# Four edits at the MLP openings of a two-layer trunk: where operand T4 is summed, from which pair the modulation steps run, which engine adds some squares, and where one statistic stands

## The chip, the cores and the metric

One core of a Trainium2 chip runs the program. The metric is the device time of one execution in microseconds (us), as a median over runs. TensorE (PE) multiplies matrices, VectorE (DVE), ScalarE (ACT) and GpSimd (POOL) work on tiles, and SyncE (SP) issues most of the DMAs. Each engine runs its own instructions in a fixed order and waits on semaphores for the others.

## The reference

A trunk of two layers over 1024 latent tokens and 256 context tokens, width 1024. Every sub-layer is preceded by an RMSNorm with a scale and a shift that depend on a conditioning vector (the modulation), and is added with a gate that depends on it too.

```python
def rms_norm(x, g):
    y = xf * lax.rsqrt(jnp.mean(xf * xf, axis=-1, keepdims=True) + EPS)
    return y * g
def sqrelu_mlp(h, w1, w2):
    return jnp.square(jax.nn.relu(h @ w1)) @ w2
```

Layer 0 mixes with an mLSTM head group beside a gated convolution, layer 1 with attention; the MLP has 4096 hidden columns. The change lies in the two MLPs and just ahead of that of layer 0.

## The kernel before, in words

**Arithmetic.** A number is split into a high and a low part of the type fp32r (`split`: the high part by a copy, L101; the low part by a subtraction, L102), and a product takes three matmuls (`mm3`, L337 to L339). The tokens lie in three blocks: 0 and 1 hold 512 latent tokens each, 2 the 256 of the context; a tile xT holds a block with the features on the partitions, 8 chunks (kt or m) of 128.

**The first MLP matrix (fc1).** `fast_fc1` multiplies 2x2 blocks by the method of Strassen and Winograd: 7 products instead of 8. A pair p is two blocks of 128 hidden columns; there are 16. For each pair the products come in the order 1, 2, 6, 5, 7, 3, 4 (layer 0 puts 8, the context's, ahead of 4), each of 4 x 3 matmuls of 128x512. For product i the token side is an operand tb[i], a sum or a difference of quarters of the normalised tokens, made once; the weight side is a sum of raw weight blocks (`ssum` or `s`, by `comb`, L853, on DVE), split into `w` by ACT (L101) and DVE (L102). Products 1 and 2 (and 8 and 9 of the context) of the first three pairs run early, while the other operands are still being made; products 6, 5, 7, 3, 4 of pair 0 follow. `after` copies or squares the results (L950, L957, L958), combines them (`c<-c` and `c<-ps,u`, L853), and spills them to DRAM (L962, L946, on SP).

**Operand T4.** `Blocks.t4` makes tb[4] = tb[2] - tb[6] just behind product 5 of pair 0: for each of 4 chunks two subtractions and an addition on DVE (12 of L853, `c<-tb` and `c<-c`), and a split. Product 4 of pair 0 is its first user.

**Modulation of layer 1.** While fc1 of layer 0 runs, `ada_steps` (L196 on) computes the modulation of layer 1 in 12 chunks of 5 steps, 60 in all: four steps each load a quarter of 0.5 MB into the tile `araw` (L203, on SP) and add it up on DVE (two or four of L211 and L213), the fifth transposes the sums on TensorE (L218) and reduces them (L220, L221, DVE). Here `araw` has a single buffer, so each load waits until DVE is done with the quarter before. `extra` takes a step behind products 2, 5, 3 and 4 of each pair that is not early, 61 chances in all; what is left is done by `step(ada1[0], 1000)` behind fc1.

**Squares and statistics.** `Norm.square` has ACT square a chunk (L281, L284) and DVE add it up (L285); behind the eighth it splits the sum into ahi and alo (L101, L102). `Norm.stat` sums these over the partitions on TensorE with a matrix of ones (L294, L295), and ACT makes rstd of it (L297, L298). Ahead of fc1 of layer 0, a loop over the blocks 2, 0, 1 and the chunks m adds the mixer's output to the stream (`add_gated`, L348) and takes squares; the statistic of block 2 is asked for behind chunk (0, 1).

**fc2.** `fast_fc2` begins with four matmuls with a tile of zeros (L1106) that open its accumulators. Its tokens come back from DRAM, 2 MB for each of the blocks 0 and 1 (`unpark`, 4 DMAs on SP each, `xT<-park`).

**Order.** The program is written as straight code; a list scheduler in the framework then fixes each engine's order from its own model of times and the dependences. A few instructions are kept in program order (`pe_`, `dve_`, ...). So an edit at one place moves instructions at others.

Of the kernel before, what the change touches and what calls it, by code (L numbers as in the profile page):

```python
# [11 lines left out]
F32 = mybir.dt.float32  # L12
F32R = mybir.dt.float32r
AF = mybir.ActivationFunctionType
ALU = mybir.AluOpType
# [4 lines left out]
P = 128  # L20
# [26 lines left out]
def trunk(ctx, tc, a, out):  # L47
    nc = tc.nc
    sp, act, dve, pool, pe = nc.sync, nc.scalar, nc.vector, nc.gpsimd, nc.tensor

    def opened(name, bufs=1, space=None, side=None):
        kw = {"space": space} if space is not None else {}
        if side is not None:
            kw["side"] = side
        return tc.tile_pool(name=name, bufs=bufs, reuse_waits="tile", **kw)
# [13 lines left out]
    def psum():  # L69
        return ps_pool.tile([P, 512], F32, name="ps", tag="ps")  # L70


    ident = const.tile([P, P], F32, name="ident")
    make_identity(nc, ident)
    ones_f = const.tile([P, P], F32, name="ones_f")
# [148 lines left out]
    def step(it, n=1):  # L224
        for _ in range(n):
            if next(it, "end") == "end":
                return
# [290 lines left out]
    for half in (1, 0):  # L518
        n = 264
        wc = load_cols(w_in, 1024 + 264 * half, n)  # L520
        for tt in range(NTT):
# [10 lines left out]
            if half:  # L532
                gv = po[:, 248:264].rearrange("p (d f h) -> p d f h", d=2, f=2)
                bv = gbias.rearrange("p (d f h) -> p d f h", d=2, f=2)
                for f, dst in ((0, ig_all), (1, fg_all)):
                    o = dst[:, tt, :]
# [119 lines left out]
    for which, dst in ((0, qT), (1, kT)):  # L656
        for i in range(2):
            w = load_split(kt_view(w_in, which * 256 + i * P, P), [KT, P])
            for b in range(3):
                t0, n = TBS[b]  # L660
# [191 lines left out]
    def comb(out, a_, b_, op, eng=None):  # L852
        (eng or dve).tensor_tensor(out=out, in0=a_, in1=b_, op=op)  # L853
# [266 lines left out]
    class Blocks:  # L1120
# [9 lines left out]
        def temp(self):  # L1130
            return self.p.tile([P, 512], F32, name="t", tag="t", bufs=4)
# [75 lines left out]
            for k in range(4):  # L1207
                self.put(3, k, self.b22[k])

        def t4(self, hi4, lo4, temp):  # L1210

            self.tb[4] = hi4, lo4
            f = lambda ap: ap.bitcast(F32)
            for k in range(4):
                t, u = temp(), temp()
                for o, x in ((t, 0), (u, 1)):
                    comb(o, f(self.tb[2][x][:, k]), f(self.tb[6][x][:, k]), ALU.subtract)
                comb(t, t, u, ALU.add)
                self.put(4, k, t)

    act_big = lambda shape: act_pool.tile(shape, F32R, name="tb", tag="act")

# [20 lines left out]
    x2ctx, x1ctx, nctx, x0ctx, lctx, actx = (ExitStack() for _ in range(6))  # L1243
# [1 line left out]
    shift = mod[0][:, 24:32, :]  # L1245
    zctx = ExitStack()
    zero = zctx.enter_context(opened("zero", 1, side="right")).tile([P, P], F32R, name="zero")
    act.activation(out=zero, in_=ones_f, func=AF.Copy, scale=0.0)
    x1 = x_of(x1ctx, 1)
    np_ = nctx.enter_context(opened("nrm", 1, side="right"))  # L1250
    xT = [x_of(x0ctx, 0), x1, x_of(x2ctx, 2)]
# [2 lines left out]
    nbs = [Norm(np_, xT[b], b, g2, shift, tbufs=4) for b in range(3)]  # L1254
# [12 lines left out]
    blocks = Blocks(np_, g2, shift, [np_.tile([P, 512], F32, name="b11", tag="b11", bufs=4) for _ in range(4)], act_big, lambda shape: big(tbp)(shape))  # L1267
    parked2 = {}
    parked2[1], part1 = park_in_parts(1, 2)
    for b in (2, 0, 1):  # L1270
        for m in range(KT):
            py = held.pop(0) if b == 2 else psum()
            if b < 2:
                mlstm_out(b, m, py)
            add_gated(xT, b, m, py, 0, 2)
            nbs[b].square(m)
            if (b, m) == (0, 1):
                parked2[2] = park(2, 2)
                nbs[2].stat()
                h2 = nbs[2].apply()  # L1280
                x2ctx.close()
            if (b, m) == (1, 0):
                nbs[0].stat()
                blocks.first(nbs[0])
                parked2[0] = park(0, 2)
            if b == 1:
                part1(m)
                if m >= 4:
                    blocks.ahead(nbs[1], m - 4)
# [6 lines left out]
    wp, raw_tile = Later(), lambda shape, e=0: raw_pool.tile(shape, F32, name="raw", tag="raw")  # L1296
# [5 lines left out]

    def begin(p, i, room):
        if i == 5 and fourth and p == room[1] // 3:
            t4 = fourth.pop()
            blocks.t4(t4[:, 0], t4[:, 1], lambda: wp.tile([P, 512], F32, name="c", tag="c", bufs=room[2]))

    fourth = []

    def extra(p, i, room):  # L1310
        begin(p, i, room)
        if i in (2, 5, 3, 4):
            step(ada1[0])

    def end():
        blocks.put22()
        nctx.close()
        x1ctx.close()
        t4 = lctx.enter_context(opened("tb4", 1)).tile([P, 2, 4, 512], F32R, name="tb4")
        ap = actx.enter_context(opened("adp", 1, side="right"))  # L1320
        ada1.append(ada_steps(ap, 1, (4, 0, 5, 6, 1, 7, 8, 2, 9, 10, 3, 11), lambda ch: ch < 4, lambda: ap.tile([P, 2, 512], F32, name="araw", tag="araw")))
        wp.p = actx.enter_context(opened("fc1w", 1, side="right"))
        return t4
# [3 lines left out]
    fast_fc1(0, blocks, wp, hid_d, 3, raw_tile, 3, {1: stats, 3: lambda: blocks.t1(nbs[1]), 6: lambda: blocks.t3(nbs[1]), 11: lambda: fourth.append(end())},  # L1327
             (3, 2, 6, None), extra, ctx=h2, hid_c=hid_c, slots=slots)
    step(ada1[0], 1000)
    actx.close()  # L1330
    lctx.close()

# [67 lines left out]
    with opened("rope", 1, side="right") as rp:  # L1400
# [127 lines left out]
        k = 12 - TAIL  # L1528
# [16 lines left out]
    with opened("s", 2, PSUM) as scp, opened("st", 2, PSUM) as stp, opened("av", 2, PSUM) as avp, \  # L1545
# [94 lines left out]
        k = 12  # L1640
# [79 lines left out]
    def end():  # L1720
        blocks.put22()
        rctx.close()
        x1ctx.close()
        t4 = actx.enter_context(opened("tb4", 1, side="right")).tile([P, 2, 4, 512], F32R, name="tb4")
        wp.p = actx.enter_context(opened("fc1w", 1, side="right"))
        return t4

# [67 lines left out]
```

## Time and profile before

| what | value |
|---|---|
| median of 3 runs | 2891.22 us (2886.96 to 2892.35) |
| the profiled execution | 2892.08 us |
| its span | 2890.3 us |
| mean granted TensorE clock | 0.984 |
| PE busy | 2787.5 us, 96% |
| DVE, ACT, POOL busy | 70%, 52%, 24% |

A clock of 1.00 in a row is 2.4 GHz, 0.50 is 1.2 GHz. A line of a timeline has the start, the duration (of xN instructions together), the engine, the line of the code, the operation, its tiles and shapes, and in brackets the idle time of the engine before it and what ended it. Matmuls overlap, so their pitch is the distance of their starts, not their duration.

### The profile page before, as it was taken

How to read it: one execution, taken by the hardware profiler on the slowest of the kernel's cores; microseconds unless marked ns; L12 is line 12 of the kernel's file. 1: busy time of each engine (PE TensorE's matmuls, PEld its weight loads, DVE VectorE, ACT ScalarE, POOL GpSimd, SP SyncE). 2: the span in 40 equal slices, each digit the busy share in tenths (PEclk: the TensorE clock that was granted, in tenths of full speed). 3: DMA queues.
4: the chain of work that ended last, by engine and by line, in shares of the span. 5: the costliest groups of instructions: out<-in, count | busy, mean ns of one | idle time of the engine just before them, and what ended most of it. 6: DMA issues, size and time to landing. Idle time of an engine off the chain costs nothing.

```text
span 2890.3 us, 39559 instructions
## 1 busy us (share of the span) xinstructions
PE 2787.5 (96%) x14603; PEld 2307.4 (80%) x14603; DVE 2009.4 (70%) x3376; ACT 1496.9 (52%) x2576; POOL 686.8 (24%) x566
## 2 busy tenths in 40 slices
PE   7999999988999999999999989999999999999999
PEld 4788998876888888888888967777777788878887
DVE  6445581778767679778877767777755966578876
ACT  5311122765444454444556578888875655544443
POOL 2222313620000000000135545555554000000000
PEclk9999999999999999999999989999999999999999
DMA  7121652535665684324232310000025254484432
GB/s 241 51 70 42 202 157 59 177 115 151 210 182 176 190 300 159 131 81 146 100 121 77 92 41 19 15 19 19 19 74 178 84 186 155 139 295 160 146 98 106
DMA packets 194835, 360.21 MB, mean 125 GB/s; under 512 B 15206, under 2 KB 83666, under 8 KB 194642
## 3 DMA queue, kind: packets, MB, share of 16 engines
q1 hardware_dynamic: 179970, 312.59, 32.2%
q0 software_dynamic: 14672, 45.10, 6.0%
q8 instruction: 115, 1.88, 0.3%
q14 instruction: 78, 0.64, 0.1%
HBM read 260.53 MB, written 97.10 MB: 124 GB/s over the span
## 4 chain that ended last, share of the span: by engine, by line
PE 56%; DVE 7%; ACT 6%; DMA 4%; issue 2%; POOL 1%; SPq 0%; DVEq 0%; ACTq 0%; POOLq 0%
PE ps L339 14%; PE ps L338 14%; PE ps L337 14%; PE av L92 4%; PE st L92 3%; DMA araw<-in_ada_w_dram 2%; PE s L92 2%; ACT pt L92 2%; ACT pf L92 2%; ACT of L92 1%; PE ps L508 1%; PE ps L509 1%; PE ps L510 1%; DMA hid<-c 1%; DVE aacc L213 1%
## 5 line engine op out<-in xcount | busy, mean ns | idle before, releaser
L338 PE MATMUL ps<-w 128*128 128x512 f32 (+1 forms) x1152 | 424.6, 369 | 0.9 <-DVE w L102 0.9
L339 PE MATMUL ps<-w 128*128 128x512 f32 (+1 forms) x1152 | 423.7, 369 | 0.0
L337 PE MATMUL ps<-w 128*128 128x512 f32 (+1 forms) x1152 | 406.1, 369 | 1.5 <-ACT w L101 1.5
L337 PE MATMUL ps<-tb,w 128*128 128x512 f32 x883 | 349.5, 397 | 9.7 <-ACT w L101 7.8
L338 PE MATMUL ps<-tb,w 128*128 128x512 f32 x888 | 350.7, 395 | 1.9 <-DVE tb L92 1.9
L339 PE MATMUL ps<-tb,w 128*128 128x512 f32 x888 | 347.8, 395 | 0.8 <-DVE w L102 0.8
L348 DVE SCALAR_TENSOR_TENSOR xT<-ps,mod,xT 128x512 f32<-128x512 f32 (+1 forms) x392 | 256.4, 695 | 97.8 <-PE ps L339 86.0
L92 DVE TENSOR_REDUCE nm<-s 128x1 f32<-128x512 f32 x372 | 217.7, 600 | 107.1 <-PE s L92 102.1
L101 ACT CAST w<-ssum 128x512 fp32r<-128x512 f32 x253 | 153.9, 619 | 250.6 <-PE ps L339 232.2
L92 POOL TENSOR_TENSOR pt<-pf,pt 128x1024 fp32r<-128x1024 f32 x96 | 230.6, 2402 | 170.4 <-ACT pt L92 170.2
L92 PE MATMUL av<-pt,vst 128*128 128x512 f32 (+1 forms) x960 | 257.5, 394 | 0.8 <-POOL pt L92 0.8
L338 PEld LDWEIGHTS ps<-w 128*128 128x128 f32 x1152 | 216.8, 188 | 41.0 <-DVE w L102 1.3
L337 PEld LDWEIGHTS ps<-w 128*128 128x128 f32 x1152 | 216.2, 188 | 41.2 <-ACT w L101 1.8
L339 PEld LDWEIGHTS ps<-w 128*128 128x128 f32 x1152 | 216.3, 188 | 38.8
L92 PEld LDWEIGHTS av<-pt,vst 128*128 128x128 f32 (+1 forms) x960 | 159.7, 171 | 55.9 <-POOL pt L92 1.3
L337 PEld LDWEIGHTS ps<-tb,w 128*128 128x128 f32 x883 | 167.4, 190 | 46.1 <-ACT w L101 8.9
L895 POOL DMA_DIRECT2D raw<-in_mlp_w_dram x70 | 62.3, 890 | 594.9 <-DVE w L102 278.5
L92 ACT ACTIVATE pf<-st 128x1024 f32<-128x1024 f32 x160 | 164.3, 1027 | 75.4 <-PE st L92 74.2
L339 PEld LDWEIGHTS ps<-tb,w 128*128 128x128 f32 x888 | 167.9, 189 | 40.2 <-DVE w L102 2.3
L338 PEld LDWEIGHTS ps<-tb,w 128*128 128x128 f32 x888 | 168.7, 190 | 37.4 <-DVE tb L92 2.8
L213 DVE SCALAR_TENSOR_TENSOR aacc<-araw,cw,aacc 128x512 f32<-128x512 f32 x196 | 145.7, 775 | 71.5 <-DMA araw<-in_ada_w_dram 70.6
L102 DVE TENSOR_TENSOR w<-ssum,w 128x512 fp32r<-128x512 f32 x253 | 171.5, 686 | 23.9 <-ACT w L101 23.3
(387 smaller groups left out, 6581.5 us busy)
## 6 DMA issues: line engine op xcount, KB each, us to landing
hid<-c SPq DMA_DIRECT2D x224, 256.0 KB
tf<-hid SPq DMA_DIRECT2D x112, 512.0 KB
araw<-in_ada_w_dram SPq DMA_DIRECT2D x72, 512.0 KB
raw<-in_mlp_w_dram POOLq DMA_DIRECT2D x70, 512.0 KB, 4.9
park<-xT SPq DMA_DIRECT2D x32, 512.0 KB
xT<-park SPq DMA_DIRECT2D x32, 512.0 KB
w2e<-in_mlp_w_dram SPq DMA_DIRECT2D x32, 512.0 KB
w2o<-in_mlp_w_dram SPq DMA_DIRECT2D x32, 512.0 KB
```

The source lines that it names most:

```text
L92: return lambda *args, **kw: tc.keep_in_program_order(op(*args, **kw))
L101: (hi_eng or act.copy)(out=hi, in_=src)
L102: (lo_eng or pool).tensor_tensor(out=lo, in0=src, in1=hi.bitcast(F32), op=ALU.subtract)
L213: dve.scalar_tensor_tensor(out=accs[w], in0=r[:, k, :], scalar=c, in1=accs[w], op0=ALU.mult, op1=ALU.add)
L337: pe1.matmul(ps, whi, hhi, start=start, stop=False, skip_group_check=goes_on)
L338: pe.matmul(ps, whi, hlo, start=False, stop=False, skip_group_check=goes_on)
L339: pe.matmul(ps, wlo, hhi, start=False, stop=stop, skip_group_check=goes_on)
L348: dve.scalar_tensor_tensor(out=xT[b][:, m, :], in0=ps[:, 0:n], scalar=mod[layer][:, gate * 8 + m, w:w + 1], in1=xT[b][:, m, :], op0=ALU.mu ...
L508: pe.matmul(ps[:, 0:n], hhi, whi, start=kt == 0, stop=False)
L509: pe.matmul(ps[:, 0:n], hhi, wlo, start=False, stop=False)
L510: pe.matmul(ps[:, 0:n], hlo, whi, start=False, stop=kt == KT - 1)
L895: pool.dma_start(out=r, in_=kt_view(w1, (2 * p + e) * P, P))
```

## The change

1. T4 is summed on TensorE, in both layers. For each of the 4 chunks four matmuls of 128x512 add plus and minus identities times the high and low parts of tb[2] and tb[6] in a PSUM bank, and the split reads that bank. The identities are scaled by ACT (L1222). Layer 0 uses the tile `zero` as minus and fills it with zeros behind fc1 (L1333).
2. `extra` takes a modulation step only from pair 1 on. That leaves 58 chances for 60 steps: the last quarter of chunk 11 and its transposes are now taken by `step(ada1[0], 1000)`.
3. The squares of block 1 with odd m are added on POOL (four of L285).
4. The statistic of block 2, its norm and its parking are asked for behind chunk (0, 3).

```diff
-        def t4(self, hi4, lo4, temp):
+        def t4(self, hi4, lo4, signs):
             self.tb[4] = hi4, lo4
-            f = lambda ap: ap.bitcast(F32)
             for k in range(4):
-                t, u = temp(), temp()
-                for o, x in ((t, 0), (u, 1)):
-                    comb(o, f(self.tb[2][x][:, k]), f(self.tb[6][x][:, k]), ALU.subtract)
-                comb(t, t, u, ALU.add)
+                t = psum()
+                for n, (i, x) in enumerate(((2, 0), (2, 1), (6, 0), (6, 1))):
+                    pe.matmul(t, signs[i // 6], self.tb[i][x][:, k], start=n == 0, stop=n == 3)
                 self.put(4, k, t)
+    def with_signs(p, minus=None):
+        signs = [p.tile([P, P], F32R, name="plus"), minus or p.tile([P, P], F32R, name="minus")]
+        for t, v in zip(signs, (1.0, -1.0)):
+            act.mul(out=t, in_=ident, mul=v)
+        return p.tile([P, 2, 4, 512], F32R, name="tb4"), signs
...
-            nbs[b].square(m)
-            if (b, m) == (0, 1):
+            nbs[b].square(m, pool if b == 1 and m % 2 else dve)
+            if (b, m) == (0, 3):
                 parked2[2] = park(2, 2)
                 nbs[2].stat()
...
     def extra(p, i, room):
         begin(p, i, room)
-        if i in (2, 5, 3, 4):
+        if p >= 1 and i in (2, 5, 3, 4):
             step(ada1[0])
...
     step(ada1[0], 1000)
+    act.activation(out=zero, in_=ones_f, func=AF.Copy, scale=0.0)
```

**How it moves instructions, first place: ahead of block 2's statistic.** DVE before, around the split of the sum of squares of block 2 (128x256); xT_5555 is block 0.

```order
L348 SCALAR_TENSOR_TENSOR xT_5555<-ps,mod_118,xT_5555 128x512
L285 TENSOR_TENSOR acc<-acc,sq 128x256
L348 SCALAR_TENSOR_TENSOR xT_5555<-ps,mod_118,xT_5555 128x512
L285 TENSOR_TENSOR acc<-acc,sq 128x256 x3
L101 CAST ahi<-acc 128x256
L102 TENSOR_TENSOR alo<-acc,ahi 128x256
L285 TENSOR_TENSOR acc<-acc,sq 128x512
L348 SCALAR_TENSOR_TENSOR xT_5555<-ps,mod_118,xT_5555 128x512
```

DVE now (block 0 is xT_5554):

```order
L348 SCALAR_TENSOR_TENSOR xT_5554<-ps,mod_118,xT_5554 128x512
L285 TENSOR_TENSOR acc<-acc,sq 128x256
L348 SCALAR_TENSOR_TENSOR xT_5554<-ps,mod_118,xT_5554 128x512
L285 TENSOR_TENSOR acc<-acc,sq 128x256 x3
L348 SCALAR_TENSOR_TENSOR xT_5554<-ps,mod_118,xT_5554 128x512
L101 CAST ahi<-acc 128x256
L102 TENSOR_TENSOR alo<-acc,ahi 128x256
L285 TENSOR_TENSOR acc<-acc,sq 128x512
```

One more gated addition of block 0 stands ahead of the split; on TensorE, 23 more matmuls of the mixer's output stand ahead of L294, which uses it (row 2638 before, 2661 now).

**Second place: the opening of fc1.** DVE before, in products 6, 5 and 7 of pair 0:

```order
L102 TENSOR_TENSOR w<-s_6331,w 128x512
L853 TENSOR_TENSOR ssum<-raw 128x512
L853 TENSOR_TENSOR c<-tb 128x512 x6
L853 TENSOR_TENSOR s_6331<-raw,s_6331 128x512
L213 SCALAR_TENSOR_TENSOR aacc_6495<-araw,cw,aacc_6495 128x512
L102 TENSOR_TENSOR w<-ssum,w 128x512
L853 TENSOR_TENSOR c<-c 128x512 x3
L102 TENSOR_TENSOR w<-s_6331,w 128x512
L102 TENSOR_TENSOR w<-raw,w 128x512
L853 TENSOR_TENSOR c<-tb 128x512 x2
L102 TENSOR_TENSOR tb_6406<-c,tb_6406 128x512 x2
L213 SCALAR_TENSOR_TENSOR aacc_6495<-araw,cw,aacc_6495 128x512
```

DVE now, at the split of T4 (tb_6408 is tb[4], `ps` a PSUM bank):

```order
L853 TENSOR_TENSOR ssum<-raw 128x512
L102 TENSOR_TENSOR tb_6408<-ps,tb_6408 128x512
L853 TENSOR_TENSOR ssum<-ssum,raw 128x512
L853 TENSOR_TENSOR ssum<-raw 128x512
L102 TENSOR_TENSOR tb_6408<-ps,tb_6408 128x512 x2
L102 TENSOR_TENSOR w<-ssum,w 128x512
L102 TENSOR_TENSOR tb_6408<-ps,tb_6408 128x512
L213 SCALAR_TENSOR_TENSOR aacc_6613<-araw,cw,aacc_6613 128x512
```

TensorE now, behind product 5 of pair 0:

```order
L339 MATMUL ps<-tb,w 128x512
L1216 MATMUL ps<-tb,plus 128x512 x2
L1216 MATMUL ps<-tb,zero 128x512 x2
L1216 MATMUL ps<-tb,plus 128x512 x2
L1216 MATMUL ps<-tb,zero 128x512 x2
L1216 MATMUL ps<-tb,plus 128x512 x2
L1216 MATMUL ps<-tb,zero 128x512 x2
L1216 MATMUL ps<-tb,plus 128x512 x2
L1216 MATMUL ps<-tb,zero 128x512 x2
L337 MATMUL ps<-tb,w 128x512
```

The 12 combs are gone from DVE, and 16 matmuls stand in TensorE's order.

**Third place: the end of fc1 of layer 0.** TensorE before, at its last modulation transposes, some 60 rows ahead of fc2's first matmul (L1106 is row 4937):

```order
L337 MATMUL ps<-tb,w 128x512
L338 MATMUL ps<-tb,w 128x512
L339 MATMUL ps<-tb,w 128x512
L218 MATMUL ps<-ident,aacc_9599 128x128 x4
L337 MATMUL ps<-h2h,w 128x256
L338 MATMUL ps<-h2l,w 128x256
L339 MATMUL ps<-h2h,w 128x256
```

TensorE now; h2h is the context's operand, and L1106 opens fc2:

```order
L337 MATMUL ps<-tb_6408,w 128x512
L338 MATMUL ps<-tb_6408,w 128x512
L339 MATMUL ps<-tb_6408,w 128x512
L339 MATMUL ps<-h2h,w 128x256
L218 MATMUL ps<-ident,aacc_9767 128x128 x4
L1106 MATMUL ps<-w,zero 128x512 x4
L337 MATMUL ps<-w 128x256
```

DVE now, in the same stretch (`c<-c` are the combinations of pair 15's results, `w` weights of fc2):

```order
L213 SCALAR_TENSOR_TENSOR aacc_9767<-araw,cw,aacc_9767 128x512 x2
L853 TENSOR_TENSOR c<-c 128x512
L102 TENSOR_TENSOR w<-w2e,w 128x512
L853 TENSOR_TENSOR c<-c 128x512 x3
L102 TENSOR_TENSOR w<-tf,w 128x512
L213 SCALAR_TENSOR_TENSOR aacc_9767<-araw,cw,aacc_9767 128x512 x2
L102 TENSOR_TENSOR w<-w2o,w 128x512
L213 SCALAR_TENSOR_TENSOR aacc_9767<-araw,cw,aacc_9767 128x512 x2
L220 TENSOR_REDUCE asum<-ps 128x4
```

SP now, in the same stretch (xT_9895 and xT_9894 are the blocks 1 and 0 for fc2, `hid` and `hidc` spills of pair 15):

```order
L92 DMA xT_9895<-park_5577 128x1024 x3
L962 DMA hid_6024<-c 128x512
L203 DMA araw<-in_ada_w_dram 128x2x512
L962 DMA hid_6024<-c 128x512
L946 DMA hidc_6028<-c 128x512
L962 DMA hid_6024<-c 128x512 x4
L1043 DMA tf<-hid_6021 128x1024
L92 DMA xT_9894<-park_5872 128x1024 x4
L203 DMA araw<-in_ada_w_dram 128x2x512
L92 DMA xT_9899<-park_5680 128x512 x4
```

The last transposes now stand between fc1 and fc2, behind two pairs of L213 at the end of DVE's pair 15, and the last `araw` stands on SP behind the spills and four transfers of xT.

## Rows read from the trace of the kernel before

**Rows 1.** The page: busy time and share of the span of each engine.

```profile
PE 2787.5 (96%) x14603; PEld 2307.4 (80%) x14603; DVE 2009.4 (70%) x3376; ACT 1496.9 (52%) x2576; POOL 686.8 (24%) x566
```

**Rows 2.** Busy time by stretch, from the end of the mixer's output (620) to the opening of fc1 of layer 0: columns PE, PEld, DVE, ACT, POOL busy (and instructions), clock, DMA share, GB/s.

```profile
620.00:640.00 20.00, 16.90 (x70) 13.16 (x70) 19.26 (x27) 14.42 (x26) 8.96 (x6) 0.83 0.21 72
...
660.00:680.00 20.00, 17.30 (x84) 13.74 (x83) 19.99 (x35) 13.11 (x24) 1.77 (x2) 0.91 0.40 126
```

**Rows 3.** Timeline of PE at the statistic of block 2.

```profile
582.56 0.55 PE L294 MATMUL ps<-ahi,ones_r 128*128 128x256 f32 x1 [5.61 <-DVE ahi L101]
...
586.75 0.63 PE L337 MATMUL ps<-mT,whi 128*128 128x512 f32 x1
587.18 0.44 PE L338 MATMUL ps<-mT,whi 128*128 128x512 f32 x1
```

**Rows 4.** Timeline of PE in the opening of fc1 of layer 0: the matmuls that it waited for, and two at the end of a stretch at the lower clock.

```profile
629.36 0.79 PE L337 MATMUL ps<-tb 128*128 128x512 f32 x1 [3.07 <-ACT tb L101]
...
668.66 0.50 PE L92 MATMUL ps<-tb,w 128*128 128x512 f32 x1 [1.92 <-ACT w L101]
...
677.54 0.50 PE L339 MATMUL ps<-tb,w 128*128 128x512 f32 x1 [0.78 <-DVE w L102]
...
687.94 0.79 PE L337 MATMUL ps<-tb,w 128*128 128x512 f32 x1 [5.05 <-ACT w L101]
...
692.38 0.63 PE L337 MATMUL ps<-tb,w 128*128 128x512 f32 x1
...
700.14 0.63 PE L218 MATMUL ps<-ident,aacc 128*128 128x128 f32 x4 [1.29 <-DVE aacc L213]
...
709.48 0.50 PE L337 MATMUL ps<-tb,w 128*128 128x512 f32 x1 [2.76 <-ACT w L101]
```

**Rows 5.** Timeline of DVE in the same stretch: the combs of T4, the weight sum and the low part that follow them, and two waits for modulation loads.

```profile
671.92 3.69 DVE L853 TENSOR_TENSOR c<-tb 128x512 f32<-128x512 f32 x6
...
677.40 1.89 DVE L853 TENSOR_TENSOR c<-c 128x512 f32<-128x512 f32 x3
...
680.41 1.29 DVE L853 TENSOR_TENSOR c<-tb 128x512 f32<-128x512 f32 x2
...
684.69 0.69 DVE L853 TENSOR_TENSOR c<-c 128x512 f32<-128x512 f32 x1
...
686.55 0.69 DVE L853 TENSOR_TENSOR ssum<-ssum,raw 128x512 f32<-128x512 f32 x1
...
697.97 0.75 DVE L213 SCALAR_TENSOR_TENSOR aacc<-araw,cw,aacc 128x512 f32<-128x512 f32 x1 [4.54 <-DMA araw<-in_ada_w_dram]
...
716.54 1.41 DVE L213 SCALAR_TENSOR_TENSOR aacc<-araw,cw,aacc 128x512 f32<-128x512 f32 x2 [3.09 <-DMA araw<-in_ada_w_dram]
```

**Rows 6.** Timeline of SP's queue: the issues of the two loads that the last two rows of group 5 waited for.

```profile
692.86 0.38 SPq L203 DMA_DIRECT2D araw<-in_ada_w_dram  x1
...
711.58 0.39 SPq L203 DMA_DIRECT2D araw<-in_ada_w_dram  x1
```

**Rows 7.** POOL: the group of its 128x512 multiplications in fp32 (L789), by form (busy us, mean ns); and the timelines of DVE and POOL at one place before fc1 of layer 1, where both work on SBUF.

```profile
L789 POOL TENSOR_TENSOR gso<-gso,hs 128x512 f32<-128x512 f32 x10 | 12.7, 1276 | 6.3 <-ACT rs L791 4.9 <-DVE hs L777 1.0 <-ACT mT L101 0.4
...
2197.70 2.40 POOL L102 TENSOR_TENSOR wlo<-raw,whi 128x1024 fp32r<-128x1024 f32 x1 [2.60 <-ACT whi L101]
...
2198.26 2.38 DVE L285 TENSOR_TENSOR acc<-acc,sq 128x512 f32<-128x512 f32 x1 [0.75 <-ACT sq L284]
```

**Rows 8.** Layer 1: timeline of PE at its last wait in the opening of fc1, and of DVE at its first T4 combs.

```profile
2284.88 0.50 PE L337 MATMUL ps<-tb,w 128*128 128x512 f32 x1 [0.76 <-ACT u L950]
2285.22 0.40 PE L338 MATMUL ps<-tb,w 128*128 128x512 f32 x1
2285.45 0.40 PE L339 MATMUL ps<-tb,w 128*128 128x512 f32 x1
...
2284.79 3.09 DVE L853 TENSOR_TENSOR c<-tb 128x512 f32<-128x512 f32 x5
```

**Rows 9.** The end of fc1 of layer 0, timeline of PE: the last modulation transposes, fc1's last matmul, fc2's first.

```profile
1054.52 0.60 PE L218 MATMUL ps<-ident,aacc 128*128 128x128 f32 x4
...
1065.95 0.28 PE L339 MATMUL ps<-h2h,w 128*128 128x256 f32 x1
1066.07 1.09 PE L1106 MATMUL ps<-w,zero 128*128 128x512 f32 x4
```

**Rows 10.** The same place, timeline of DVE: the wait for the last quarter, and the last combination of pair 15.

```profile
1049.52 0.75 DVE L213 SCALAR_TENSOR_TENSOR aacc<-araw,cw,aacc 128x512 f32<-128x512 f32 x1 [2.35 <-DMA araw<-in_ada_w_dram]
...
1070.76 0.68 DVE L853 TENSOR_TENSOR c<-c 128x512 f32<-128x512 f32 x1
```

**Rows 11.** The same place, timeline of SP's queue: the last modulation load, four transfers of xT, and the spills of pair 15 and the load behind them.

```profile
1045.39 0.38 SPq L203 DMA_DIRECT2D araw<-in_ada_w_dram  x1
...
1062.10 3.50 SPq L92 DMA_DIRECT2D xT<-park  x4
1065.99 0.96 SPq L962 DMA_DIRECT2D hid<-c  x2
...
1071.75 0.39 SPq L1043 DMA_DIRECT2D tf<-hid  x1
```

**Rows 12.** Busy time by stretch from the end of fc1 on, columns as in group 2.

```profile
1060.00:1080.00 20.00, 20.00 (x147) 18.98 (x146) 13.57 (x22) 13.30 (x24) 0.00 (x0) 1.00 1.03 377
1080.00:1420.00 340.00, 340.00 (x1794) 291.25 (x1793) 275.45 (x451) 151.55 (x266) 0.00 (x0) 1.00 0.36 127
```

More of the change, by code (lines that the diff above doesn't have):

```diff
@@ L1247, in trunk @@
     zero = zctx.enter_context(opened("zero", 1, side="right")).tile([P, P], F32R, name="zero")
-    act.activation(out=zero, in_=ones_f, func=AF.Copy, scale=0.0)
     x1 = x_of(x1ctx, 1)
@@ L1304, in begin @@
         if i == 5 and fourth and p == room[1] // 3:
-            t4 = fourth.pop()
-            blocks.t4(t4[:, 0], t4[:, 1], lambda: wp.tile([P, 512], F32, name="c", tag="c", bufs=room[2]))
+            t4, signs = fourth.pop()
+            blocks.t4(t4[:, 0], t4[:, 1], signs)
     fourth = []
@@ L1318, in end @@
         x1ctx.close()
-        t4 = lctx.enter_context(opened("tb4", 1)).tile([P, 2, 4, 512], F32R, name="tb4")
+        t4 = with_signs(lctx.enter_context(opened("tb4", 1)), zero)
         ap = actx.enter_context(opened("adp", 1, side="right"))
@@ L1723, in end @@
         x1ctx.close()
-        t4 = actx.enter_context(opened("tb4", 1, side="right")).tile([P, 2, 4, 512], F32R, name="tb4")
+        t4 = with_signs(actx.enter_context(opened("tb4", 1, side="right")))
         wp.p = actx.enter_context(opened("fc1w", 1, side="right"))
```

## The prediction

> **What bounds the kernel now.** The page first: TensorE is busy for 2787.5 us of the 2890.3 us span, DVE for 70% [rows 1]. So TensorE sets the end, and an edit is worth what it takes from TensorE's idle time or its time at the lower clock, or adds to its work. DVE counts only where TensorE waits for it. I therefore looked for TensorE's waits, and at DVE and SP only there.
>
> At the statistic of block 2 TensorE stands for 5.61 us until DVE has split the sum of squares, and then runs at the lower clock: the matmul at 586.75 comes 0.43 us before the next [rows 3]. In the opening of fc1 of layer 0 DVE is busy for 19.99 of 20 us [rows 2], and TensorE waits 1.92, 0.78, 5.05, 1.29 and 2.76 us for weights, or modulation sums, that DVE makes or makes possible [rows 4], 11.80 us together. The longest lies behind the T4 combs [rows 5]. In the same stretch 3.07 us go at the first product of block 1 [rows 4]. From the opening of fc1 of layer 1 on hardly anything is left to win: the last wait there is 0.76 us [rows 8]. And the end of fc1 of layer 0 is seamless: last modulation transposes at 1054.52, last fc1 matmul at 1065.95, first fc2 matmul at 1066.07 [rows 9], then 340.00 busy of 340 us [rows 12]. That last place is the one to watch.
>
> **The change part by part.**
>
> *A, the statistic of block 2.* TensorE now has 24 matmuls of the mixer's output (m = 2 and 3) ahead of the one that waits, 24 x 0.23 (the pitch of [rows 8]) = 5.5 us of work that is there anyway and fills the 5.61 us. Without the gap the clock has no reason seen here to fall: of the ten matmuls from 582.9 to 587.18, at a pitch of 0.43 instead of 0.23, 2 us come back [rows 3]. The split itself waits for one more gated addition, whose matmuls are ahead of it on TensorE, so a part of a microsecond may remain. Value -7.5, bounds -8 and -4. Parking and the context's norm start some 6 us later; block 2's operand is first used by products 8 and 9 in fc1, some 50 us on, which covers that.
>
> *B, squares on POOL.* Four additions leave DVE (0.6 us each) for POOL, where the nearest form takes 1.28 us [rows 7]. The last of them, which completes the sum, stands on POOL behind four splits (7.2 us) and a weight issue; DVE's split of the sum follows it, and on TensorE the block's statistic stands behind more of the context's short matmuls than before, about 2 us later by their number. So T2, T3 and T6 begin later by that, at a time when TensorE has products of the early pairs to do. The gap of 3.07 us waits for ACT, and stays. Against it speaks how the two engines meet: while POOL split 128x1024 for 2.40 us, an addition of DVE that took 0.69 elsewhere took 2.38 [rows 7]. If each POOL square holds DVE so for 1.28 us, four cost DVE 5.1 us and spare it 2.4, net 2.7, in a stretch where DVE is full (19.26 of 20 [rows 2]). Value +0.5, bounds -1 and +3. The Trainium skill, "GPSIMD Engine Reference", section Specifications, says the same of its cause: the two engines share their SBUF interfaces, and contend when DVE's instruction has two SBUF inputs; by it the upper bound, +3, would stand in place of +0.5 and the sum would be 2.5 us higher.
>
> *C, the opening of layer 0.* T4 took DVE 3.69 + 1.89 + 1.29 + 0.69 = 7.6 us [rows 5], less 0.3 for overlaps. The modulation steps of pair 0 took some 5 of L211 and L213, 0.75 us each [rows 5], 3.5 us more. All that stood ahead of the sum that the wait of 5.05 us ended on. With about 10 us off DVE there, that wait goes, with 2.2 us at the lower clock behind it (11 matmuls up to 692.38 [rows 4], 0.2 us each). Most of 0.78 goes too. The wait of 1.92 lies ahead of T4 and stays in part. Those of 1.29 and 2.76 do not go: DVE stands for `araw` for 4.54 and 3.09 us, each 5 us behind the issue (692.86 to 697.97, 711.58 to 716.54 [rows 5, 6]); with one buffer that wait moves with the steps to pair 1. Of 11.8 idle and about 5.3 at the lower clock, I leave 4.5 and 3.2, so 9.4 come back. TensorE pays 16 matmuls of 128x512 at 0.23, the pitch of [rows 8]: 3.7. Value -5.7, bounds -10 (everything but the 1.92 gone) and 0 (the waits on `araw` take the place of those on DVE).
>
> *D, the opening of layer 1.* The same 16 matmuls, 3.7 us. The combs stand on DVE from 2284.79 on, when TensorE's last wait, 0.76 us for ACT, is just over [rows 8], so nothing waits for them. Half of the matmuls can lie in that 0.76. Value +2.9, bounds +2 and +4.
>
> *E, the last two steps.* The last transposes now stand on TensorE between fc1's last matmul and fc2's first; everything of fc2 is queued behind them, and needs nothing of them. In the time of before, TensorE arrives at 1066.2. The third quarter's additions stand on DVE behind the combinations of pair 15, the last of which began at 1070.76 [rows 10], and a split: they run at about 1071.9 to 1073.3. Only then is the single buffer free. On SP the last load also stands behind pair 15's spills, a load of `tf` at 1071.75, and four transfers of xT that take 3.50 us to issue [rows 11], so it goes out at about 1075.8. From issue to use a load took 4.1 [rows 10, 11] to 5.1 us [rows 5, 6]: landing at 1080 to 1081, two additions of 0.7, and TensorE goes on at about 1082. With a delay of one microsecond for the 2 MB of xT just ahead of it (377 GB/s move there at a DMA share of 1.03 [rows 12]), the stall is 17 us. Behind waits of 5 us TensorE lost 1.9 to 2.2 us at the lower clock; I add 2. Nothing gives this back: TensorE is busy for all of the next 340 us [rows 12]. Value +19. Lower bound: xT does not stand in the way, load at 1073.3, 4.1 us, 1.4 us: a stall of 12.6, with clock +14. Upper bound: xT's 2 MB, 5.6 us at 377 GB/s, are drained first, and the third load is late by 2: 24 us, with clock +26.
>
> The Trainium skill, "DMA: Bandwidth & Descriptors", section Anatomy of one DMA, gives an estimate for a transfer: 2.0 us and the bytes at 436 GB/s, 3.2 us for 0.5 MB. The rows show 4.1 to 5.1, so the trace does not agree; by the page E would be 2 us less.
>
> **Sum.** -7.5 + 0.5 - 5.7 + 2.9 + 19 = +9.2 on the profiled execution of 2892.1 us: 2901.3. That execution lies 0.9 us over the median, so 2900.4.
>
> **The rivals.**
>
> *R1, no stall at the end.* The order on TensorE is fixed, but the last load could land before TensorE arrives, if quarter three is done inside pair 15 and SP is early. For it: before, the last transposes came 11.5 us ahead of fc1's end. Against it: two more steps, and the additions stand behind combinations that need the last product. A to D alone: -9.8, 2881.4, faster.
>
> *R2, short stall, full relief.* E at its lower bound, +14, and C at -9, A -7.5, B +0.5, D +2.5: +0.5, 2891.7. For it: DVE and SP reach the end of pair 15 earlier if TensorE does. It decides when the last load goes out before 1074.
>
> *R3, long stall.* E at +26 with C at -5: +17, 2908, slower. For it: the DMA share at 1060 to 1080; against it: TensorE, which needs weights and hidden columns from the same DMA engines there, is busy for 20.00 of 20 us.
>
> *R4, T4 gives nothing back.* The waits in the opening were for `araw` and weights, not for T4: C 0 and B +3 with E +19: +17, 2908, slower. It decides if DVE still has no free time behind product 5.
>
> **How the numbers follow.** The forecast has 0.48, R1 0.15, R2 0.22, R3 0.09, R4 0.06. A measurement of this kernel tells about 0.2%, 5.8 us, from no change: faster is under 2885.4, slower over 2897.0. Of the forecast, with its spread of some 6 us, three quarters are slower and the rest the same; R1 is faster; of R2 three quarters are the same and the rest faster; R3 and R4 are slower. Faster 0.20, same 0.29, slower 0.51. The range: to R1's 2881 at the low end would take in all; I leave half of R1 out, 2883, and above R3 and R4, 2912.
>
> **What would show it.** A: no wait of over 1 us ahead of the 128x256 statistic. C: no wait of 5 us behind product 5 of pair 0, and DVE with free time there. D: no more waits in layer 1's opening, 16 more matmuls. E: one wait of 13 to 24 us for `aacc` at the last transposes, a lower clock behind it, and DVE waiting for `araw` just before. I am wrong if that wait is under 10 us, or if the opening keeps its 12 us of waits.

## The result, and the profile after

The changed kernel takes 2916.66 us (2911.75 to 2922.1, 4 runs) against 2890.56 us on the same chip: ratio 1.0089 (95% interval 1.0077 to 1.010), 26 us slower. The forecast was 2900.4 us, slower; the time lies above its range. The execution profiled after is the slowest of the four, 2922.1 us with a span of 2920.3, so the ledger below sums to 30 us, 4 more than the medians differ.

TensorE's waits of the kernel after, from its timeline, and fc2's first matmuls:

```profile
583.86 0.38 PE L294 MATMUL ps<-ahi,ones_r 128*128 128x256 f32 x1 [1.15 <-DVE ahi L101]
600.54 0.79 PE L294 MATMUL ps<-ahi,ones_r 128*128 128x512 f32 x1 [2.20 <-DVE ahi L101]
625.80 0.79 PE L337 MATMUL ps<-tb 128*128 128x512 f32 x1 [3.42 <-ACT tb L101]
...
667.64 0.50 PE L339 MATMUL ps<-tb,w 128*128 128x512 f32 x1 [1.86 <-DVE w L102]
698.64 0.50 PE L339 MATMUL ps<-tb,w 128*128 128x512 f32 x1 [1.08 <-DVE w L102]
732.83 0.39 PE L339 MATMUL ps<-h2h,w 128*128 128x256 f32 x1 [2.19 <-DVE w L102]
...
928.93 0.50 PE L337 MATMUL ps<-tb,w 128*128 128x512 f32 x1 [1.58 <-DVE c L853]
973.96 0.39 PE L339 MATMUL ps<-h2h,w 128*128 128x256 f32 x1 [1.88 <-DVE w L102]
...
1029.74 0.39 PE L339 MATMUL ps<-h2h,w 128*128 128x256 f32 x1 [2.55 <-DVE w L102]
...
1068.17 0.28 PE L339 MATMUL ps<-h2h,w 128*128 128x256 f32 x1
1092.14 1.09 PE L218 MATMUL ps<-ident,aacc 128*128 128x128 f32 x4 [23.69 <-DVE aacc L213]
1092.88 2.06 PE L1106 MATMUL ps<-w,zero 128*128 128x512 f32 x4
```

Read beside [rows 3] and [rows 4], the wait of 5.61 us has shrunk to 1.15, that of 5.05 us is gone, and 3.42 stands for 3.07. New are the waits of 1.6 to 2.6 us from 928 on, where the kernel before had hardly any, and the one of 23.69 us at the last transposes; [rows 9] have none there. The four L1106 take 2.06 us instead of 1.09, at a granted clock of 0.50 from 1092 to 1095; with the transposes and what follows that is some 1.5 us.

DVE of the kernel after, from its timeline, just ahead of three of the waits from 928 on, and at the wait of 23.69 us:

```profile
925.53 2.74 DVE L213 SCALAR_TENSOR_TENSOR aacc<-araw,cw,aacc 128x512 f32<-128x512 f32 x4 [5.31 <-DMA araw<-in_ada_w_dram]
...
972.55 0.75 DVE L213 SCALAR_TENSOR_TENSOR aacc<-araw,cw,aacc 128x512 f32<-128x512 f32 x1 [3.05 <-DMA araw<-in_ada_w_dram]
...
1025.14 2.08 DVE L213 SCALAR_TENSOR_TENSOR aacc<-araw,cw,aacc 128x512 f32<-128x512 f32 x3 [3.17 <-DMA araw<-in_ada_w_dram]
...
1068.70 1.54 DVE L213 SCALAR_TENSOR_TENSOR aacc<-araw,cw,aacc 128x512 f32<-128x512 f32 x2 [2.87 <-DMA araw<-in_ada_w_dram]
...
1071.36 1.89 DVE L853 TENSOR_TENSOR c<-c 128x512 f32<-128x512 f32 x3
...
1076.81 1.54 DVE L213 SCALAR_TENSOR_TENSOR aacc<-araw,cw,aacc 128x512 f32<-128x512 f32 x2 [2.19 <-DMA araw<-in_ada_w_dram]
...
1090.45 1.54 DVE L213 SCALAR_TENSOR_TENSOR aacc<-araw,cw,aacc 128x512 f32<-128x512 f32 x2 [7.42 <-DMA araw<-in_ada_w_dram]
```

SP of the same run, from its timeline (w2e and w2o are fc2's weights):

```profile
1050.96 0.57 SPq L1034 DMA_DIRECT2D w2e<-in_mlp_w_dram  x1
...
1052.60 0.94 SPq L1034 DMA_DIRECT2D w2e<-in_mlp_w_dram  x2
1053.65 1.97 SPq L1034 DMA_DIRECT2D w2o<-in_mlp_w_dram  x3
1055.66 0.52 SPq L1034 DMA_DIRECT2D w2e<-in_mlp_w_dram  x1
1056.23 0.43 SPq L1034 DMA_DIRECT2D w2o<-in_mlp_w_dram  x1
...
1058.19 0.38 SPq L203 DMA_DIRECT2D araw<-in_ada_w_dram  x1
...
1070.27 0.38 SPq L203 DMA_DIRECT2D araw<-in_ada_w_dram  x1
...
1076.89 2.65 SPq L92 DMA_DIRECT2D xT<-park  x4
1080.48 0.38 SPq L203 DMA_DIRECT2D araw<-in_ada_w_dram  x1
```

So DVE stands for a modulation load for 3 to 5 us shortly before it makes what TensorE waits for at 928.93, 973.96 and 1029.74. The last three loads take 10.5, 6.5 and 10.0 us from issue to use, where those of [rows 5, 6, 10, 11] took 4.1 to 5.1. They are serial: each goes out only after the additions that free the buffer. The first of the three goes out behind eight loads of fc2's weights, 4 MB, the last behind four transfers of xT, 2 MB.

Where TensorE gains and loses, stretch by stretch. The stretches before and after run between the same matmuls or the same copies of products (L950), so a column is a difference of two starts:

| stretch | forecast | measured |
|---|---|---|
| start of the execution to 546 | | +1.1 |
| A, to block 0's statistic (605.96, now 600.54) | -7.5 | -6.5 |
| B, to product 1's copy of the first opening pair (674.00, now 671.47) | +0.5 | +2.9 |
| C, to the copy at 698.88 (now 691.61) | -5.7 for all of fc1 | -4.7 |
| C, to fc1's last matmul (1065.95, now 1068.17) | | +9.5 |
| E, to L1106 (1066.07, now 1092.88) | +19 | +24.6 |
| from there to 2274.88 (now 2305.62) | | +3.9 |
| D, 2274.88 to 2596.60 (now 2305.62 to 2630.67) | +2.9 | +3.3 |
| from there to the end | | -4.0 |

No run ties the two late rows without a letter to an edit. Over nearly the first of them (1066.07 to 2284.73) the traces of the last two runs of the experiments, whose edits do not reach there, differ by 5.2 us, so a difference of a few us between two single executions can be chance.

So the opening won what was forecast, and by the end of fc1 more than that was lost again. Two groups of DVE from the start of fc1 to the middle of fc2's first part (640 to 1100) point to the cause; first the kernel before, then after (busy us, mean ns, idle before by releaser):

```profile
L213 DVE SCALAR_TENSOR_TENSOR aacc<-araw,cw,aacc 128x512 f32<-128x512 f32 x112 | 81.9, 748 | 59.7 <-DMA araw<-in_ada_w_dram 58.9
```

```profile
L213 DVE SCALAR_TENSOR_TENSOR aacc<-araw,cw,aacc 128x512 f32<-128x512 f32 x112 | 81.9, 749 | 74.3 <-DMA araw<-in_ada_w_dram 73.7
```

### The profile page after: what moved, and what is told of

Same layout as the page of the kernel before. It is cut to its first block, busy times and chain, and to the rows that moved or that the text cites. A ratio compares the mean times of both kernels' runs of the same rounds, so it can differ in the third digit from the quotient of the medians.

```text
span 2920.3 us, 39610 instructions
## 1 busy us (share of the span) xinstructions
PE 2794.3 (96%) x14635; PEld 2320.6 (79%) x14635; DVE 1996.4 (68%) x3348; ACT 1495.5 (51%) x2580; POOL 692.1 (24%) x570
## 5 line engine op out<-in xcount | busy, mean ns | idle before, releaser
L213 DVE SCALAR_TENSOR_TENSOR aacc<-araw,cw,aacc 128x512 f32<-128x512 f32 x196 | 146.0, 778 | 86.2 <-DMA araw<-in_ada_w_dram 85.5
```

The costliest lines, as they stand in the source:

```text
L213: dve.scalar_tensor_tensor(out=accs[w], in0=r[:, k, :], scalar=c, in1=accs[w], op0=ALU.mult, op1=ALU.add)
```

## The experiments

The theory after the result: the modulation loads, serial in one buffer, pace DVE, and with it all of fc1 of layer 0; whatever the opening wins is waited away later, and a later start of the steps ends in the stall. The rivals are named with each run. The median of the kernel before in the same batch is given as "beside". A lead is what a trace is ahead of the kernel before at the same copy of a product, less what it was ahead at 560, before anything that the edits touch.

**Steps from pair 0 again.**

```diff
-        if p >= 1 and i in (2, 5, 3, 4):
+        if i in (2, 5, 3, 4):
```

> The changed kernel with its second edit undone: modulation steps from pair 0 again, so 61 chances for 60 steps. Theory (the steps alone cost time: a stall at the end of fc1 of layer 0, and waits on late modulation loads in pairs 10 to 15, because DVE stands in its fixed order for araw): no wait at the last transposes, no waits of over 1 us between 900 and 1060, and what the other edits gain in the opening less 3.7 us of T4 in layer 1 stays: 2883 to 2888 us, that is 3 to 7 us under the kernel before. Rival (the waits of pairs 10 to 15 come from the other edits, which shift the products against the loads): the end is seamless too, but 5 to 8 us of waits remain between 900 and 1060: 2891 to 2895.

Measured: 2885.89 beside 2891.46, ratio 0.9980 (0.9972 to 0.9989). No wait at the transposes, and one over 1 us, 1.58, between 900 and 1060. From its timeline:

```profile
1050.02 0.60 PE L218 MATMUL ps<-ident,aacc 128*128 128x128 f32 x4
...
1061.59 1.09 PE L1106 MATMUL ps<-w,zero 128*128 128x512 f32 x4
```

The three other edits are worth 5.6 us; the steps cost 31 us on top of them. As the theory had it. Two waits of 3.24 and 2.12 us near 730 remain, at weights and modulation sums.

**The steps alone**, the same line changed in the kernel before.

> The kernel before with the second edit alone: steps from pair 1 on. Theory: the whole loss and more: a wait of 20 to 26 us at the last transposes, 5 to 8 us of waits between 900 and 1060, and 1 to 4 us won in the opening, since the steps of pair 0 are gone: 2913 to 2922. Rival (the waits of pairs 10 to 15 come from the other edits): the same stall, none of those waits: 2908 to 2913.

Measured: 2925.91 beside 2891.46, ratio 1.0121 (1.0105 to 1.0136): +34 us, more than theory and rival. A wait of 25.61 us at the transposes, with four of 0.9 to 2.0 us between 900 and 1060, which the rival did not have:

```profile
1093.76 1.09 PE L218 MATMUL ps<-ident,aacc 128*128 128x128 f32 x4 [25.61 <-DVE aacc L213]
```

**61 chances from pair 1 on.**

```diff
-        if p >= 1 and i in (2, 5, 3, 4):
+        if p >= 1 and i in (2, 5, 3, 4) or p in (1, 2, 3) and i == 7:
```

> The changed kernel with three more chances for a step (behind product 7 of pairs 1 to 3), 61 in all from pair 1 on, so that the last transposes come some 60 matmuls ahead of the end of fc1. Theory: the stall of 23.7 us goes whole, with its 1 to 2 us at the lower clock, and the waits between 900 and 1060 go or shrink, since the steps are back in the places of before: 2884 to 2889. Rival (a late end of the modulation is a matter of DMA and DVE time, not of the count of chances): a stall of 8 us or more remains: 2897 or more.

Measured: 2898.56 beside 2891.46, ratio 1.0021 (1.0012 to 1.0031). The stall is gone, but the time is 13 us over the run with steps from pair 0: the expectation missed. TensorE now waits in the middle of fc1, some pairs behind the extra steps; its longest wait, from the timeline of this run:

```profile
826.24 0.80 PE L337 MATMUL ps<-tb,w 128*128 128x512 f32 x1 [4.06 <-DVE c L853]
```

Just ahead of it DVE stood for a modulation load for 5.20 us, to 824.17. The lead is 9.7 us at 812, and at 916 the run is 0.6 behind. With the same loads in fewer pairs the loss has moved from the end into the middle.

**T4 on TensorE alone**, in both layers (the first edit as in the diff ahead).

> The kernel before with the first edit alone: T4 on TensorE in both layers. Theory (the wait of 5 us in the opening was for the T4 combs on DVE): that wait goes with its 2 us at the lower clock, 32 matmuls cost 7.3 us, about 3.3 of them in layer 1 with nothing won there: 2888 to 2892, no change. Rival (the wait was for modulation loads and weights): the wait stays and the 7.3 us are added: 2896 to 2898.

Measured: 2895.63 beside 2891.46, ratio 1.0013 (1.0004 to 1.0022): between the two. The wait of 5.05 us at 687.94 is gone, and at the copy of 698.88 this run is 4.7 us ahead, with the 16 matmuls paid. But from its timeline:

```profile
711.50 0.50 PE L337 MATMUL ps<-tb,w 128*128 128x512 f32 x1 [1.91 <-ACT u L950]
...
735.82 1.12 PE L218 MATMUL ps<-ident,aacc 128*128 128x128 f32 x4 [2.04 <-DVE aacc L213]
...
794.58 0.39 PE L339 MATMUL ps<-h2h,w 128*128 128x256 f32 x1 [1.76 <-DVE w L102]
...
860.70 0.50 PE L337 MATMUL ps<-tb,w 128*128 128x512 f32 x1 [2.31 <-DVE c L853]
```

At 1043 it is 6.3 us behind. So T4 alone gives its gain back and more, without any change to the steps, in an execution 3.1 us over this run's median.

**Without three of four loads**, the kernel before and the changed one. Layer 1's modulation is computed from the first quarter of each chunk alone.

```diff
-                r = raw_tile() if raw_tile else p.tile([P, 2, 512], F32, name="araw", tag="araw", bufs=2)
-                sp.dma_start(out=r, in_=...)
+                if q == 0 or not raw_tile:
+                    r = raw_tile() if raw_tile else p.tile([P, 2, 512], F32, name="araw", tag="araw", bufs=2)
+                    sp.dma_start(out=r, in_=...)
```

> The kernel before with three of four loads of layer 1's modulation left out: each chunk loads its first quarter and uses it for all four, so the modulation of layer 1 is another, while every addition on DVE and every transpose stays. It is the base for the next run. Theory (DVE's waits for modulation loads, 70 us of them in fc1 of layer 0, pace DVE but are mostly hidden): the waits of TensorE at 700.14 and 709.48 go or shrink, and so do the small ones up to 927, 6 to 9 us together: 2882 to 2886. Rival (those waits have other causes): 2889 to 2892.

> The changed kernel with the same loads left out, additions and transposes kept; the last transposes still stand between fc1 and fc2. Theory (both losses, the stall and what is given back from pair 2 on, come from the loads in their single buffer): no wait of over 3 us at the last transposes, no waits of over 1 us from 740 to 1060, and the change is then a gain: 2879 to 2884, 2 to 6 us under the run beside it with the edits undone. Rival (the order of the additions on DVE and the transposes' place on TensorE cost the time even without loads): a stall of 7 us or more and 2890 or more.

Measured, beside 2892.65: 2881.05 for the kernel before (0.9953, 0.9941 to 0.9965), 2872.80 for the changed one (0.9927, 0.9915 to 0.9940), both below what the theory expected. Without three of four loads the change is a gain of 8 us, and there is no wait at the last transposes, which stand where they stood. From the changed one's timeline, where each line number is one higher:

```profile
1044.36 0.60 PE L219 MATMUL ps<-ident,aacc 128*128 128x128 f32 x4
1044.72 1.18 PE L1107 MATMUL ps<-w,zero 128*128 128x512 f32 x4
```

Busy time by stretch of both, columns as in group 2 ahead, first the kernel before, then the changed one:

```profile
660.00:740.00 80.00, 72.02 (x334) 58.65 (x333) 75.83 (x127) 40.00 (x72) 8.25 (x9) 0.94 0.51 155
740.00:1050.00 310.00, 310.00 (x1653) 266.21 (x1652) 217.93 (x357) 148.39 (x257) 18.54 (x21) 1.00 0.48 155
```

```profile
660.00:740.00 80.00, 76.30 (x351) 62.62 (x352) 71.69 (x119) 41.17 (x76) 7.95 (x9) 0.98 0.53 157
740.00:1050.00 310.00, 310.00 (x1667) 266.71 (x1666) 216.34 (x354) 147.56 (x255) 17.66 (x20) 1.00 0.50 160
```

From 740 to 1050 TensorE never waits in either. With the loads it is busy for 306.56 us of that stretch in the kernel before and 299.21 in the changed one. In the opening without loads the kernel before still waits 4.74 us at the same matmul as at 687.94, and the changed one does not: that wait was for T4. The lead of the changed one over the other is 7.9 us at the copy of 697.63, and still 7.5 us at 1030. The loads left out cost the kernel before 11.6 us, and the changed one 44 to 46, by its medians in two batches. They also take 18 MB of traffic away (a DMA share of 0.48 to 0.50 from 740 to 1050, instead of 0.58 to 0.62); that the waits come from DVE standing at the loads, and not from the traffic, rests on the rows of DVE shown with the result.

**The last load on POOL's queue.**

```diff
-                sp.dma_start(out=r, in_=...)
+                (pool if raw_tile and ch == 11 and q == 3 else sp).dma_start(out=r, in_=...)
```

> The changed kernel with the very last modulation load issued on POOL's queue instead of SP's, so that it does not stand behind the spills, tf and four transfers of xT there; it still waits for the single buffer. In the changed kernel it went out at 1080.48, 2.1 us after the buffer came free, and was used 9.97 us later. Theory (the bytes of xT on the shared DMA engines hold it, not the place in the queue): 1 to 4 us off the stall of 23.7 us: 2913 to 2917. Rival (the place on SP, with the 2 MB issued ahead of it, makes the length): a load of 5 us right after the buffer is free, a stall of 16 to 17.5 us: 2909 to 2911.

Measured: 2912.52 beside 2892.65, ratio 1.0063 (1.0051 to 1.0075). From this run's timelines of POOL, DVE and PE:

```profile
1076.21 0.70 POOL L203 DMA_DIRECT2D araw<-in_ada_w_dram  x1 [64.33 <-DMA hid<-c]
...
1085.27 1.54 DVE L213 SCALAR_TENSOR_TENSOR aacc<-araw,cw,aacc 128x512 f32<-128x512 f32 x2 [4.35 <-DMA araw<-in_ada_w_dram]
...
1086.95 1.09 PE L218 MATMUL ps<-ident,aacc 128*128 128x128 f32 x4 [22.27 <-DVE aacc L213]
```

It goes out 0.3 us after the additions that free the buffer and still takes 9.1 us: 1.4 us off the stall, as the theory had it; the time lies half a microsecond under the theory's range. The Trainium skill, "DMA: Bandwidth & Descriptors", section Issuing engines are not separate DMA queues, says that DMAs of all issuing engines run on the same 16 engines and interleave; the trace agrees: 9.1 us from POOL beside 10.0 from SP, with 2.75 MB issued on SP in the 6 us ahead of either.

**Block 0's transfers behind the last transposes.**

```diff
+    for q in range(4):
+        dve.tensor_copy(out=xT[0][:, 2 * q, 0:1], in_=mod[1][:, 44, 0:1])
```

> The changed kernel with four one-column copies from the last modulation into the tile of block 0, so that its four transfers (2 MB) are issued behind the last transposes; every other instruction keeps its place. Theory (the 2 MB, issued right ahead of the last modulation load, make it take 10 us instead of 5, and their issues on SP keep it back by 2 us): it goes out right behind the third quarter's additions, takes 4.5 to 5.5 us, and the stall is 16 to 18.5 us instead of 23.7: 2909 to 2912. Rival (the engines are full there whatever stands ahead, since spills and weights of fc2 move too): 9 us or more, a stall of 21 us or more, 2913 to 2917.

Measured: 2912.38 beside 2892.00, ratio 1.0068 (1.0056 to 1.0080). The issue on SP, the additions on DVE and the wait on PE, from this run's timelines:

```profile
1072.36 0.38 SPq L203 DMA_DIRECT2D araw<-in_ada_w_dram  x1
...
1079.06 1.54 DVE L213 SCALAR_TENSOR_TENSOR aacc<-araw,cw,aacc 128x512 f32<-128x512 f32 x2 [1.66 <-DMA araw<-in_ada_w_dram]
...
1080.74 1.09 PE L218 MATMUL ps<-ident,aacc 128*128 128x128 f32 x4 [20.00 <-DVE aacc L213]
```

The load takes 6.7 us instead of 10.0, and goes out at once. So block 0's 2 MB cost it 3.3 us, less than expected. The issue wins another 2.1 us, but the additions of the third quarter come 1.7 us later against TensorE than in the changed kernel, and the stall is 20.0 us, between theory and rival. What is left is the two serial loads (6.1 and 6.7 us) with three pairs of additions and the combinations of pair 15 between them.

**The statistic alone**, `(b, m) == (0, 3)` for `(0, 1)` in the kernel before.

> The kernel before with the fourth edit alone: block 2's statistic behind chunk (0, 3). Theory (it fills the gap of 5.6 us ahead of it, and the gain lasts to fc1's opening, but there waits on modulation loads in fc1 take part of it back): 2 to 7 us under the kernel before: 2885 to 2890. Rival (the gain is kept whole, since DVE's waits on loads begin only after it): 7 to 8 us: 2884 to 2885.

Measured: 2889.49 beside 2892.00, ratio 0.9990 (0.9981 to 0.9999): 2.5 us, the low end of the theory. The wait falls to 1.09 us; the next one, at block 0's statistic, grows from 1.18 to 2.20. The lead is 5.8 us at block 0's statistic, 9.5 at 728 and 5.7 at 1043: in this trace fc1 takes nothing of it back, against the theory; the lead at the end of the program is 3.4.

**The squares alone**, on POOL in the kernel before.

> The kernel before with the third edit alone: four squares of block 1 added on POOL. Theory (DVE's four additions are hidden, and POOL's hold DVE about as long): within 2 us of the kernel before, 2889.5 to 2893.5. Rival (POOL's additions hold DVE's, block 1's operands come late): 3 to 5 us over it, 2894.5 to 2896.5.

Measured: 2891.98 beside 2892.00, ratio 0.9999 (0.9990 to 1.0007). No difference, as the theory had it.

**Steps from pair 0, and T4 on TensorE in layer 0 alone.** The changed kernel with its second edit undone; layer 1's T4 is made by the combs of before (`signs` is None there).

```diff
-        t4 = with_signs(actx.enter_context(opened("tb4", 1, side="right")))
+        t4 = actx.enter_context(opened("tb4", 1, side="right")).tile([P, 2, 4, 512], F32R, name="tb4"), None
```

> The changed kernel with two edits undone: steps from pair 0 again, and T4 of layer 1 on DVE as before; T4 of layer 0 stays on TensorE, squares and statistic stay as changed. Theory (T4 on TensorE in layer 1 only adds its 16 matmuls): 2.5 to 4 us under the run with only the steps undone (2885.9): 2881.5 to 2883.5. Rival (DVE's combs in layer 1 delay weights there as in layer 0): the same as that run or slower, 2885 to 2888.

Measured: 2880.91 beside 2892.65, ratio 0.9957 (0.9945 to 0.9969), 5 us under the run with only the steps undone. In the opening of layer 1 (2274.88 to 2299.89) the trace of that run loses 3.4 us and this one nothing: T4 on TensorE in layer 1 only adds. This version beats both kernels.

**The same with two half buffers for the loads.**

```diff
+                    r = [raw_tile() for k in range(2)]
+                    for k in range(2):
+                        sp.dma_start(out=r[k], in_=a["ada_w"][layer][q * 256 + k * P:q * 256 + (k + 1) * P, ch * 512:(ch + 1) * 512])
...
+ lambda: ap.tile([P, 512], F32, name="araw", tag="araw", bufs=2)
```

> The run best1 (2880.9: the changed kernel with steps from pair 0 and layer 1's T4 on DVE) with each quarter of the modulation loaded as two halves in two buffers of half the size, so that in the same memory one half is under way while DVE adds the other. Theory (the serial loads, one quarter after the other with 5 us from issue to use, still cost best1 what the runs without loads show, up to 10 us): DVE's waits for araw shrink by a third or more, 2 to 5 us less: 2876 to 2879. Rival (best1's steps are hidden already, or more and smaller transfers cost as much): 2880 to 2883.

Measured: 2883.46 beside 2892.00, ratio 0.9971 (0.9961 to 0.9981), not better than the run before. DVE's waits for `araw` (640 to 1100; L211 and L213, here L217 and L219) are 52.5 us instead of 63.3, so they shrink by a sixth, not a third; the two buffers are emptied within one step, and the next loads still start only then. Nor did the 11 us less of waiting on DVE shorten the program, so TensorE did not wait for these.

**The rest of fc1 in all traces.** What each trace gains or loses against the kernel before from 674.00 to the copy at 698.88, and from there to fc1's last matmul (us):

| run | opening | rest of fc1 |
|---|---|---|
| the changed kernel | -4.7 | +9.5 |
| the same, last load on POOL | -4.7 | +6.4 |
| the same, block 0's transfers late | -4.7 | +4.2 |
| the same, 61 chances from pair 1 on | -4.8 | +9.1 |
| the steps alone | +0.6 | +5.2 |
| T4 alone | -5.2 | +11.0 |
| the statistic alone | -1.5 | -0.3 |
| the squares alone | -1.0 | +0.1 |
| steps from pair 0 | -4.8 | +2.3 |
| steps from pair 0, T4 in layer 0 alone | -4.7 | +0.1 |
| the same, two half buffers | -5.1 | -0.8 |
| without three of four loads: before, changed | 0.0, -4.8 | -11.9, -11.0 |

The first three rows hold nearly the same program up to there, so they show how far single executions differ. The theory's "whatever the opening wins is waited away later" holds where the steps start at pair 1, and for T4 alone; with all three other edits and the steps from pair 0, half of what the opening wins or more stays (2.3 and 0.1 us lost of 4.8 and 4.7). Why T4 alone loses so much more was not settled. Nor do the edits add up: alone they are worth +4.2, +34.5, 0.0 and -2.5 us, 36 together, and the change is 26.

## Why the prediction was wrong

- What bounds the kernel, and the one place to watch: right. E, the stall at the last transposes, is the largest loss.
- **C failed in kind**, and it alone lies outside its bounds: -5.7 forecast for all of fc1, with 0 as the worst, and +4.8 measured. The opening gave 4.7 as the steps of the sum said: the wait of 5.05 was T4's, since it goes with T4 alone, and 4.74 of it stay without three of four loads. What failed is that the sum put nothing, without a reason, for the rest of fc1. The 60 steps, pressed into the pairs from 1 on, cost 4 to 10 us there (the five traces with steps from pair 1 and all loads), where the same other edits with steps from pair 0 lose 0.1 to 2.3. By the medians 61 chances from pair 1 take 12.7 us more than steps from pair 0, with no stall in either. DVE's order is fixed and holds 48 serial loads, so DVE stands at loads that are not there, and TensorE behind it. I had the rows for it (4.54 and 3.09 us of waits for `araw` in [rows 5]) and put it into C's worse bound as zero, not as a loss. The runs with three of four loads left out show it: there the lead stays. Nor did the second edit gain anything in the opening, where I had counted 3.5 us of DVE time for it: -4.7 with it and -4.8 without.
- **E's size failed**: 19 forecast, 24.6 measured. The step was "from issue to use a load took 4.1 to 5.1 us" with one microsecond for the 2 MB ahead of it. The last load took 10.0 us, 3.3 of them for block 0's transfers by the run that moves these, 1.6 more since other traffic still moved (6.7 there). The third load took 6.5, and its additions came 2.7 us later than worked out, measured from the end of fc1, because the second load, at 10.5 us behind 4 MB of weights, was late too. The order on SP, which I had costed, was right, and is worth 1.4 us. My upper bound, +26, held; the value I took lay too near to the rows of the opening, though the DMA share of 1.03 in [rows 12] spoke for the other end. The 3.2 us that the prediction quotes from the Trainium skill, "DMA: Bandwidth & Descriptors", section Anatomy of one DMA, stand there for transfers that GpSimd issues, and SP issued these.
- A: 7.5 forecast, 6.5 in its stretch. 1.0 us went to the next statistic, 1.2 stayed in the wait, just over the 1 us that was to show A. Alone it is worth 2.5 us by the medians; that fc1 takes the rest back is not shown (its trace loses nothing there).
- B: +0.5 forecast, +2.9 in that stretch; alone no difference in the time. In the same stretch the trace of the statistic alone loses 1.9, behind its wait of 2.20 us, and that of the squares alone 1.1, with the wait of 3.4 us in place of 3.07 that every run with the squares on POOL has. The squares get that back in the opening, where a wait of 3.11 us stands for the one of 5.05.
- D: +2.9 against +3.3. Right.
- The waits of 928 to 1030 in the changed kernel are shown to come from the loads: DVE stands at one shortly ahead of each of the three longest, they go without three of four loads, and nearly go with steps from pair 0. Why they fall just there was not settled.

## What to carry to other kernels

Before a gain at one place is summed, look for a paced chain further on in the same stage: a serial load per step, in one buffer, with the consumer in a fixed order, can turn a lead into a wait, as for T4 alone; whether it does depends on the other edits and takes a run to find out. To start such a chain later saved nothing at its start here and cost 4 to 10 us on its way; where two steps were left over for its end, 21 to 27 us more, with its last loads in a burst of other transfers there. And take a transfer's time from rows of the traffic in which it will run.

## What was not expected of the hardware

A load of 0.5 MB took 3.6 to 6.0 us from issue to use inside fc1 (kernels before and after, where DVE stood waiting for it). At the end of fc1 it took 6.0 to 6.7 us with up to 1.25 MB issued in the 6 us ahead of it, and 9.1 to 11.2 us with 2.75 to 4 MB, whether SP or POOL issued it.
